# Second half of x turned by transposing transfers instead of TensorE

## The chip, the cores and the metric

The kernel runs on 1 core of one Trainium2 chip. The metric is the time of one execution on the device in microseconds (us). Before the change it is 2121.41 us, the median of 3 runs (2120.31 to 2122.93). Engines: PE is TensorE (matmuls, weight loads apart as PEld), DVE is VectorE, ACT is ScalarE, POOL is GpSimd, SP is SyncE, which here only issues transfers. A "q" behind a name (ACTq) is that engine's issuing of transfers.

## The reference

One layer of an encoder, sequence 1024, width 2048, all in float32:

```
h      = rmsnorm(x, pre_g) * (1 + scale(c)) + shift(c)
proj   = h @ w_in                     # 2048 x 4608: q, k, v, gate_a, u, gate_p
y_a    = windowed_attention(q, k, v) * silu(gate_a)
y_p    = multiscale_pool(u) * silu(gate_p)
g      = sigmoid(h @ w_merge + b_merge)          # 2048 x 4096
merged = g_a * (y_a @ w_branch_attn) + g_p * (y_p @ w_branch_pool)
out    = x + gate(c) * rmsnorm(merged @ w_out, post_g)
```

The change touches how h gets its second half of columns, channels 1024 to 2047: x must be normalised (a factor per row, rstd), turned so that channels lie on partitions, and modulated (a factor and a shift per channel).

## The kernel before

**Products.** Every float32 factor is split into a high part (ACT, L92) and a low part (DVE, L93), and a product is three matmul passes: high x high, high x low, low x high. On top of that the blocks are multiplied by Strassen's scheme (Winograd's form): a pair of 128-column blocks of weights takes seven products, named after the moving operand B11, T3, T2, B21, T4, T1, B22, in the accumulators X, V and Z (L207). Each product is 12 matmuls of 128x512 over four k tiles. A pair of blocks is the unit of the order: `run` goes through its seven pieces and at some of them (`every`) takes one step off a list of side work, `side`.

**Stages.** The input projection with w_in and w_merge goes over 34 pairs, for the first 1024 channels of h first (pass 1), with the partial results in DRAM, and then for the second (pass 2). The first half of x is turned at the start by PE. While pass 1 goes on, its side lists do other work: the modulation vectors, the gate, the bias lines, and sums of w_out's blocks for the last stage (`weight_sums`: four loads, four sums on DVE, four stores to ws_d; `with_sums` puts the loads at one step and the sums three steps on). The last ten pairs of pass 1, from about 535 to 705 us, hold the stage that is changed: x's second half, in 16 tiles of 128 rows x 512 columns, and the weight sums 9 to 15.

**The stage.** In step n tile n is fetched on ACT's queue (L832) and tile n - 5 is turned: ACT scales it by rstd (L837), PE makes four 128x128 transposes into a bank of PSUM (L840), and ACT copies them to H, the stage's buffer of turned x (L841). Then come 16 steps of modulation (L462 on ACT, L464 on DVE), four of preparation (`pre`, L107), and in the last pair the operand fills for pass 2 begin. The weight sums share the ring of eight tiles (`xt2`) with x, and start when its tiles come free.

**Order and queues.** Each engine has one queue and keeps its order. A scheduler orders the instructions by the order of the code. Side steps are put behind the latest matmul and the latest low part by `placed`. Halves of weights (whi, wlo) have four buffers each, so the half for a product is made when the product four earlier lets its buffer go. In a pair ACT also copies X to seed Z (L233) and reads the accumulators (L218, L256, L279). POOL issues the side loads and side stores; SP issues the weights and results of the products.

Of the kernel before, what the change touches and what calls it, by code (L numbers as in the profile page):

```python
# [11 lines left out]

F32 = mybir.dt.float32
F32R = mybir.dt.float32r
AF = mybir.ActivationFunctionType
ALU = mybir.AluOpType
AX = mybir.AxisListType
# [3 lines left out]
P = 128  # L21
# [8 lines left out]
NB = S // P  # L30
# [6 lines left out]
HALF = KT // 2  # L37
# [5 lines left out]
def encoder_layer(ctx: ExitStack, tc: tile.TileContext, x, c, table, w_ada, b_ada, pre_g,  # L43
# [15 lines left out]
    nc = tc.nc  # L59
    x = x[0]  # L60
# [4 lines left out]
    def pool(name, bufs=1, **kw):  # L65
        return tc.tile_pool(name=name, bufs=bufs, reuse_waits="tile", **kw)
# [10 lines left out]
    def uid(s):  # L77
        cnt[0] += 1
        return f"{s}_{cnt[0]}"

    def bank(tag, name="b"):
        return psum.tile([P, 512], F32, tag=tag, name=uid(name), bufs=1 if tag in SEEDED else 2)
# [23 lines left out]
    def sub(o, a, b, eng=None):  # L106
        (eng or nc.vector).tensor_tensor(o, a, b, ALU.subtract)  # L107
# [3 lines left out]
    side_load = side_store = nc.gpsimd.dma_start  # L111

    ident = const.tile([P, P], F32, name="ident")
# [7 lines left out]
    sc = const.tile([P, KT], F32, name="sc")  # L121
# [200 lines left out]
    mid = ExitStack()  # L322
# [8 lines left out]
    for r0, src in ((0, c[0]), (16, b_ada[0, 0:D]), (32, b_ada[0, D:2 * D]),  # L331
                    (48, pre_g[0]), (64, b_merge[0]), (96, pool_scale[0])):
        n = src.shape[0] // P
# [125 lines left out]
    def modulate(eng, t, k):  # L459
        a, b = modc[:, 1, k:k + 1], modc[:, 0, k:k + 1]  # L460
        if eng is nc.scalar:
            eng.activation(t, t, AF.Identity, scale=a, bias=b)  # L462
        else:
            eng.tensor_scalar(t, t, a, b, op0=ALU.mult, op1=ALU.add)  # L464

    op = new_op()
    PAIRS = (NIN + 2 * D) // 256
# [187 lines left out]
    side = deque([lambda: None] * (7 * RAMP))  # L655
# [22 lines left out]
    parts = {}  # L678
# [8 lines left out]
                  if i < RAMP - 1 else None)  # L687
    flush()
    ramp.close()
    xa = mid.enter_context(pool("xa", 5))  # L690
    i = RAMP

    def pass1(n, side, every=(0, 2, 4, 6), then=None):
# [65 lines left out]
    def weight_sums(n, tile_):  # L759

        q, j = n // 4, n % 4
        r0, n0 = (q // 2 * 8 + 2 * j) * P, q % 2 * 512
        t = [[tile_() for _ in range(2)] for _ in range(2)]
        for k in range(2):
            for h_ in range(2):
                side_load(t[k][h_], w_out[r0 + k * P:r0 + (k + 1) * P, h_ * 1024 + n0:h_ * 1024 + n0 + 512])

        def sums():
            (a11, a21), (a12, a22) = t
            sub(a21, a11, a21)  # L770
            sub(a22, a22, a21)
            add(a11, a11, a22)
            sub(a12, a12, a22)
            for n, s_ in enumerate((a11, a21, a12, a22)):
                side_store(ws_d[q][j * P:(j + 1) * P, n * 512:(n + 1) * 512], s_)

        return sums

    def with_sums(steps, first, stride, ns, tile_):

        got = {}

        def begin(f, n):
            got[n] = weight_sums(n, tile_)
            f()

        def end(f, n):
            f()
            got.pop(n)()

        for i_, n in enumerate(ns):
            a, b = first + i_ * stride, first + i_ * stride + 3
            steps[a] = lambda f=steps[a], n=n: begin(f, n)
            steps[b] = lambda f=steps[b], n=n: end(f, n)
        return steps

    steps = [s_ for m in (2, 3) for s_ in modulation_steps(m)]
# [8 lines left out]
    halves = deque()  # L806
    side = deque(with_sums(steps, 14, 6, range(9), in_ring))
# [13 lines left out]
    mid = ExitStack()  # L821
# [1 line left out]
    H = [sp.tile([P, HALF, 512], F32, name=f"H{s}") for s in range(2)]  # L823
    h = {HALF + k: [H[s][:, k] for s in range(2)] for k in range(HALF)}

    def x_tile():
        return sp.tile([P, 512], F32, tag="xt2", name=uid("xt"), bufs=8)

    def fetch_x(si, q):
        xt = x_tile()  # L830
        c0 = 1024 + q * 512
        nc.scalar.dma_start(xt, x[si * P:(si + 1) * P, c0:c0 + 512])  # L832
        return xt

    def turn_x(si, q, xt):
        with tc.issue_after(last_hi[0].ins):
            nc.scalar.activation(xt, xt, AF.Copy, scale=rstd[:, si:si + 1])  # L837
        pt = bank("sc")
        for j in range(4):
            nc.tensor.transpose(pt[:, j * P:(j + 1) * P], xt[:, j * P:(j + 1) * P], ident)  # L840
        nc.scalar.activation(H[si // 4][:, 4 * q:4 * q + 4, (si % 4) * P:(si % 4 + 1) * P],  # L841
                             pt.rearrange("p (k t) -> p k t", k=4), AF.Copy)

    held, AHEAD = {}, 5

    def x_step(n):
        if n < 2 * NB:
            held[n] = fetch_x(n // 2, n % 2)
        if n >= AHEAD:
            turn_x((n - AHEAD) // 2, n % 2 ^ AHEAD % 2, held.pop(n - AHEAD))  # L850

    steps = [lambda n=n: x_step(n) for n in range(2 * NB + AHEAD)]
    steps += [lambda k=k, s=s: modulate((nc.scalar, nc.vector)[s], h[k][s], k) for k in h for s in range(2)]
    h1, h2 = ({j: h[HALF + ktile(kh, j)] for j in range(4)} for kh in range(2))
    t2 = {}

    def pre(j):
        t2[j] = pre_op(j, h1, h2, x_tile)

    steps += [lambda j=j: pre(j) for j in range(4)]  # L860
    every = (0, 1, 3, 4, 6)
    steps += [lambda: None] * (len(every) * (PAIRS - i) - len(steps))
    side = deque(with_sums(steps, 2 * NB + 1, 4, range(9, 16), x_tile))

    def put_all(o, name, h1, h2, t2):
        for j in range(4):
# [21 lines left out]
    side = deque()  # L888
# [730 lines left out]
```

## Time and profile before

| | |
|---|---|
| median of 3 runs | 2121.41 us |
| the profiled execution | 2121.76 us |
| its span, first to last instruction | 2119.6 us |
| PE busy | 2076.9 us, 98% |
| DVE busy | 1502.2 us, 71% |
| ACT busy | 1087.1 us, 51% |
| POOL busy | 195.8 us, 9% |
| mean granted clock of TensorE | 0.998 |

The span is measured inside the execution; 2.2 us lie around it. Durations in the trace are of that one execution. A timeline row merges like instructions: start, length from the first's start to the last's end, and a count; rows of PE overlap, since matmuls are pipelined, so strides between starts say more than lengths.

### The profile page before, as it was taken

Reading aid. Unit: us, or ns where it says so; the run is one execution under the profiler, and the core shown is the slowest. Engines: PE = TensorE matmul, PEld = TensorE weight load, DVE = VectorE, ACT = ScalarE, POOL = GpSimd, SP = SyncE. Lnnn points to the kernel's source line nnn. Section 1 sums busy time; section 2 is a strip of 40 time slices with the busy share of each in tenths; the row PEclk is TensorE's granted clock in tenths of the full one; section 3 lists DMA queues with packets and bytes.
Section 4 is the critical chain, followed back from the end, with each engine's and each line's share of the span. In section 5 each row is a group of like instructions: output and inputs, shape, how many; then the busy total and the mean of one; then the engine's idle time right before and its main releaser. Section 6 shows DMA issues by size and latency. Waiting matters only on the chain.

```text
span 2119.6 us, 28981 instructions
## 1 busy us (share of the span) xinstructions
PE 2076.9 (98%) x9628; PEld 1710.3 (81%) x9628; DVE 1502.2 (71%) x2701; ACT 1087.1 (51%) x2007; POOL 195.8 (9%) x424
## 2 busy tenths in 40 slices
PE   5999999999999999999999999999999999999997
PEld 3688888888888888888888888788888887888886
DVE  6788577775456866777776678757857977556568
ACT  6664444443564636777675333333645645545343
POOL 1402132221022100000000000000000000000012
PEclk9999999999999999999999999999999999999999
DMA  9868688885566565455544676575565646588358
GB/s 343 279 226 311 235 287 293 282 292 172 173 211 230 185 191 185 158 172 186 180 163 147 214 231 209 183 221 177 189 209 184 209 134 203 189 283 288 97 175 306
DMA packets 268390, 455.62 MB, mean 215 GB/s; under 512 B 23594, under 2 KB 119986, under 8 KB 268240
## 3 DMA queue, kind: packets, MB, share of 16 engines
q1 hardware_dynamic: 234016, 345.58, 50.2%
q0 software_dynamic: 30256, 100.85, 14.0%
q10 hardware_dynamic: 3968, 7.34, 1.1%
q8 instruction: 76, 1.25, 0.3%
q14 instruction: 74, 0.61, 0.1%
HBM read 321.53 MB, written 134.24 MB: 215 GB/s over the span
## 4 chain that ended last, share of the span: by engine, by line
PE 92%; DMA 4%; DVE 2%; ACT 1%; issue 1%; DVEq 0%; SPq 0%; ACTq 0%
PE Z L207 31%; PE X L207 21%; PE V L207 21%; PE OUT L1306 13%; DMA ada<-in_w_ada_dram 1%; DMA xt<-in_x_dram 1%; PE PT L987 1%; DVE po L1520 1%; PE SCORE L965 0%; PE SCORE L964 0%; PE SCORE L966 0%; PE PV L999 0%; PE PV L997 0%; PE PV L998 0%; PE GEMV L428 0%
## 5 line engine op out<-in xcount | busy, mean ns | idle before, releaser
L92 ACT ACTIVATE whi<-raw 128x512 fp32r<-128x512 f32 (+1 forms) x537 | 321.0, 601 | 467.8 <-PE Z L207 265.1
L93 DVE TENSOR_TENSOR wlo<-raw,whi 128x512 fp32r<-128x512 f32 (+1 forms) x537 | 348.4, 652 | 139.2 <-PE Z L207 79.4
L93 DVE TENSOR_TENSOR wlo<-wr,whi 128x512 fp32r<-128x512 f32 x112 | 76.5, 689 | 83.7 <-ACT whi L92 83.7
L92 ACT ACTIVATE whi<-wr 128x512 fp32r<-128x512 f32 x112 | 69.9, 628 | 111.2 <-PE OUT L1306 105.4
L104 DVE TENSOR_TENSOR u<-V,u 128x512 f32<-128x512 f32 x90 | 62.1, 690 | 73.6 <-PE V L207 73.2
L92 ACT ACTIVATE whi<-ws 128x512 fp32r<-128x512 f32 (+1 forms) x90 | 54.1, 601 | 106.5 <-PE V L207 104.0
L104 DVE TENSOR_TENSOR raw<-raw,raw 128x512 f32<-128x512 f32 x78 | 53.8, 690 | 70.8 <-DMA raw<-in_w_merge_dram 41.4
L207 PE MATMUL Z<-B22h,whi 128*128 128x512 f32 x334 | 91.3, 392 | 0.7 <-ACT u L256 0.7
L207 PE MATMUL X<-B11h,whi 128*128 128x512 f32 x334 | 91.7, 392 | 0.0
L207 PE MATMUL Z<-T1h,wlo 128*128 128x512 f32 x334 | 90.4, 390 | 1.0 <-DVE wlo L93 1.0
L207 PE MATMUL V<-T4h,whi 128*128 128x512 f32 x334 | 91.3, 392 | 0.0
L207 PE MATMUL V<-T3h,whi 128*128 128x512 f32 x334 | 91.3, 393 | 0.0
L207 PE MATMUL Z<-T1h,whi 128*128 128x512 f32 x334 | 91.3, 391 | 0.0
L207 PE MATMUL V<-T4l,whi 128*128 128x512 f32 x334 | 90.9, 390 | 0.0
L207 PE MATMUL X<-B21h,whi 128*128 128x512 f32 x334 | 90.8, 391 | 0.0
L207 PE MATMUL X<-B11l,whi 128*128 128x512 f32 x334 | 90.8, 390 | 0.0
L207 PE MATMUL Z<-T2h,whi 128*128 128x512 f32 x334 | 90.7, 391 | 0.0
L207 PE MATMUL X<-B11h,wlo 128*128 128x512 f32 x334 | 90.6, 390 | 0.0
L207 PE MATMUL V<-T3h,wlo 128*128 128x512 f32 x334 | 90.6, 390 | 0.0
L207 PE MATMUL Z<-B22l,whi 128*128 128x512 f32 x334 | 90.5, 390 | 0.0
L207 PE MATMUL V<-T3l,whi 128*128 128x512 f32 x334 | 90.5, 390 | 0.0
L207 PE MATMUL X<-B21h,wlo 128*128 128x512 f32 x334 | 90.4, 390 | 0.0
(418 smaller groups left out, 5112.3 us busy)
## 6 DMA issues: line engine op xcount, KB each, us to landing
part<-part_d SPq DMA_DIRECT2D x136, 256.0 KB, 4.1
raw<-in_w_merge_dram SPq DMA_DIRECT2D x64, 512.0 KB, 5.4
raw<-in_w_in_dram SPq DMA_DIRECT2D x60, 512.0 KB, 4.5
ada<-in_w_ada_dram POOLq DMA_DIRECT2D x96, 256.0 KB, 6.2
proj_d<-part SPq DMA_DIRECT2D x68, 256.0 KB, 2.2
gada<-in_w_ada_dram POOLq DMA_DIRECT2D x32, 512.0 KB, 5.8
gt<-proj_d SPq DMA_DIRECT2D x64, 256.0 KB, 3.3
wr<-ws_d SPq DMA_DIRECT2D x32, 512.0 KB, 4.8
```

The source lines that it names most:

```text
L92: last_hi[0] = nc.scalar.activation(hi, src, AF.Copy)
L93: last_split[0] = nc.vector.tensor_tensor(lo, src, f32(hi), ALU.subtract)
L104: (eng or nc.vector).tensor_tensor(o, a, b, ALU.add)
L207: last_mm[0] = nc.tensor.matmul(ps, w_[:, i], op[mov][j][m_], start=fresh and i == 0 and n == 0, stop=i == nj - 1 and n == 2, skip_group_c ...
L987: nc.tensor.transpose(pt[:, i * P:(i + 1) * P], p[:, i * P:(i + 1) * P], ident)
L1306: nc.tensor.matmul(banks[t], m_[:, ts_], w_, start=fresh and j == 0 and n == 0, stop=j == KS - 1 and n == 2, skip_group_check=True)
L1520: last_lo[0] = nc.vector.scalar_tensor_tensor(o_, o_, s_[:, 2:3], rows_x[si][n], op0=ALU.mult, op1=ALU.add)
```

## The change

- A tile of x is now fetched by POOL's queue. ACT scales it as before, then copies it as 16-bit words with the low words of all elements in front of the high ones (a `COPY` of 128 x 2 x 512), and issues a transposing transfer (`DMA_TRANSPOSE`) of those words into a third tile of 128 x 8 x 128 words. DVE joins low and high words back into float32 in H (`join_x`, a copy of 128 x 4 x 128 x 2 words). The transposes on PE and ACT's copy out of PSUM are gone.
- The stage's 50 steps are laid out by a table: tile n is fetched in step 3n/2 (rounded down), turned four steps later, joined two steps after that. Modulation and preparation follow in free steps, the preparation in steps 40 to 43.
- The weight sums 9 to 15 get four tiles of their own (`ws2`), start at step 4 instead of 17 and come every 6 steps instead of 4; the four sums are spread over two steps.
- The ring of side loads in the stage before (`xa`) has seven tiles instead of five, and the DMA scratch of POOL's transfers is 8192 bytes per partition, half of the default.

```diff
-    xa = mid.enter_context(pool("xa", 5))
+    xa = mid.enter_context(pool("xa", 7))
...
-        def sums():
+        def sums(parts=(0, 1)):
             (a11, a21), (a12, a22) = t
-            sub(a21, a11, a21)
-            sub(a22, a22, a21)
+            if 0 in parts:
+                sub(a21, a11, a21)
+                sub(a22, a22, a21)
+            if 1 not in parts:
+                return
             add(a11, a11, a22)
             sub(a12, a12, a22)
...
+    def x_tile(shape=(P, 512), dt=F32):
+        return sp.tile(list(shape), dt, tag="xt2", name=uid("xt"), bufs=8)
...
-    def turn_x(si, q, xt):
+    def fetch_x(n):
+        si, q = n // 8 * 4 + n % 4, n // 4 % 2
+        held[n] = x_tile()
+        side_load(held[n], x[si * P:(si + 1) * P, 1024 + q * 512:1536 + q * 512])
+
+    def turn_x(n):
+
+        si, xt = n // 8 * 4 + n % 4, held.pop(n)
         with tc.issue_after(last_hi[0].ins):
             nc.scalar.activation(xt, xt, AF.Copy, scale=rstd[:, si:si + 1])
-        pt = bank("sc")
-        for j in range(4):
-            nc.tensor.transpose(pt[:, j * P:(j + 1) * P], xt[:, j * P:(j + 1) * P], ident)
-        nc.scalar.activation(H[si // 4][:, 4 * q:4 * q + 4, (si % 4) * P:(si % 4 + 1) * P],
-                             pt.rearrange("p (k t) -> p k t", k=4), AF.Copy)
...
+        words = x_tile((P, 2, 512), U16)
+        nc.scalar.copy(words, xt.bitcast(U16).rearrange("p (n h) -> p h n", h=2))
+        turns[n] = x_tile((P, 8, P), U16)
+        nc.scalar.dma_start(turns[n], words.rearrange("p h n -> p (h n)"), transpose=True)
+
+    def join_x(n):
+        s, q, t0 = n // 8, n // 4 % 2, n % 4 * P
+        nc.vector.tensor_copy(
+            H[s][:, 4 * q:4 * q + 4, t0:t0 + P].bitcast(U16).rearrange("p k (t h) -> p k t h", h=2),
+            turns.pop(n).rearrange("p (h k) t -> p k t h", h=2))
...
+    AHEAD, LAG = 4, 2
+    work = [[] for _ in range(len(every) * (PAIRS - i))]
+    for n in range(16):
+        work[AHEAD + 3 * n // 2 + LAG].append(lambda n=n: join_x(n))
+    for n in range(16):
+        work[AHEAD + 3 * n // 2].append(lambda n=n: turn_x(n))
+    for n in range(16):
+        work[3 * n // 2].append(lambda n=n: fetch_x(n))
...
-    side = deque(with_sums(steps, 2 * NB + 1, 4, range(9, 16), x_tile))
+    side = deque(with_sums(steps, 4, 6, range(9, 16), lambda: sp.tile([P, 512], F32, tag="ws2", name=uid("ws2"), bufs=4), True))
...
-    nc = _bacc.Bacc("TRN2", target_bir_lowering=False, num_devices=1)
+    nc = _bacc.Bacc("TRN2", target_bir_lowering=False, num_devices=1, dynamic_dma_scratch_size=8192)
```

ACT's queue near the first tiles, before: loads of x, scalings, and at the end the first copy out of PSUM (b) to H. Names with "whi" are high halves of weights.

```order
L92 ACTIVATE whi_5301<-raw_4993 128x512
L832 DMA xt_5373<-in_x_dram 128x512
L279 ACTIVATE c_5226<-X_5121 128x512
L92 ACTIVATE whi_5311<-ws_5309 128x512
L837 ACTIVATE xt_5171<-xt_5171,rstd 128x512
L92 ACTIVATE whi_5355<-raw_5147 128x512
L837 ACTIVATE xt_5208<-xt_5208,rstd 128x512
L256 ACTIVATE u_1056_5266<-Z_5122 128x512
L92 ACTIVATE whi_5382<-raw_5148 128x512
L837 ACTIVATE xt_5230<-xt_5230,rstd 128x512
L233 ACTIVATE Z_5273<-X_5272 128x512
L841 ACTIVATE H_5119<-b_5295 128x4x128
```

After: each scaling is followed by the copy of words and the transposing issue.

```order
L852 ACTIVATE xt_5141<-xt_5141,rstd 128x512
L280 ACTIVATE c_5185<-Z_4964 128x512
L854 COPY xt_5277<-xt_5141 128x1024
L856 DMA_TRANSPOSE xt_5279<-xt_5277 128x8x128
L93 ACTIVATE whi_5286<-raw_5147 128x512
L219 ACTIVATE u_1046_5206<-Z_5122 128x512
L852 ACTIVATE xt_5171<-xt_5171,rstd 128x512
L854 COPY xt_5304<-xt_5171 128x1024
L93 ACTIVATE whi_5308<-raw_4993 128x512
L280 ACTIVATE c_5224<-X_5121 128x512
L856 DMA_TRANSPOSE xt_5306<-xt_5304 128x8x128
L93 ACTIVATE whi_5318<-ws_5316 128x512
```

The load and the copy to H are gone from this piece, and each tile has brought a copy of words and an issue behind its scaling, sometimes one right behind the other, sometimes with other instructions between.

DVE's queue at the same place, before: low halves of weights (wlo), combinations of weights (raw, ws), reads of results (u, p).

```order
L93 TENSOR_TENSOR wlo_5302<-raw_4993,whi_5301 128x512
L104 TENSOR_TENSOR u_1046_5206<-V_5123,u_1046_5206 128x512
L93 TENSOR_TENSOR wlo_5312<-ws_5309,whi_5311 128x512
L107 TENSOR_TENSOR ws_5495<-raw_5305 128x512
L104 TENSOR_TENSOR raw_5305<-raw_5305,raw_5306 128x4x128
L93 TENSOR_TENSOR wlo_5356<-raw_5147,whi_5355 128x512
L104 TENSOR_TENSOR p_1041_5169<-p_1041_5169,u_1056_5266 128x512
L93 TENSOR_TENSOR wlo_5383<-raw_5148,whi_5382 128x512
```

After: the first two joins (H<-xt) and the sums of w_out's blocks (ws<-ws) stand between them.

```order
L94 TENSOR_TENSOR wlo_5309<-raw_4993,whi_5308 128x512
L105 TENSOR_TENSOR u_1046_5206<-V_5123,u_1046_5206 128x512
L94 TENSOR_TENSOR wlo_5319<-ws_5316,whi_5318 128x512
L860 COPY H_5119<-xt_5279 128x4x256
L108 TENSOR_TENSOR ws_5500<-raw_5312 128x512
L105 TENSOR_TENSOR raw_5312<-raw_5312,raw_5313 128x4x128
L94 TENSOR_TENSOR wlo_5357<-raw_5147,whi_5356 128x512
L105 TENSOR_TENSOR p_1041_5169<-p_1041_5169,u_1055_5264 128x512
L860 COPY H_5119<-xt_5306 128x4x256
L108 TENSOR_TENSOR ws_1057_5269<-ws_1056_5268,ws_1057_5269 128x512
L108 TENSOR_TENSOR ws_1059_5271<-ws_1059_5271,ws_1057_5269 128x512
L94 TENSOR_TENSOR wlo_5385<-raw_5148,whi_5384 128x512
```

Each join stands ahead of the next pair's weight combinations or low halves, which now come after it.

On PE the sixteen rows of four transposes are gone, and nothing else differs but numbers in names.

## Rows read from the trace of the kernel before

**Rows 1.** The page: engines (busy us, share, instructions); the chain that ended last.

```profile
PE 2076.9 (98%) x9628; PEld 1710.3 (81%) x9628; DVE 1502.2 (71%) x2701; ACT 1087.1 (51%) x2007; POOL 195.8 (9%) x424
...
PE 92%; DMA 4%; DVE 2%; ACT 1%; issue 1%; DVEq 0%; SPq 0%; ACTq 0%
```

**Rows 2.** Table by stage: stretch, length, busy us by engine, clock, DMA share.

```profile
0.00:60.00 60.00, 35.13 (x226) 20.20 (x226) 39.26 (x108) 38.09 (x86) 14.82 (x54) 1.00 1.03 344
535.00:705.00 170.00, 170.00 (x781) 140.67 (x780) 96.91 (x154) 89.98 (x151) 30.36 (x56) 1.00 0.66 211
```

**Rows 3.** Who waited for whom, whole run: us in total, times, longest.

```profile
POOL gada L708 <- DVE gacc L712: 50.8, 14, 5.4
...
PE Z L207 <- DVE wlo L93: 1.0, 1, 1.0
```

**Rows 4.** Timeline of PE: start, us, line, operation, out<-in, shape, count.

```profile
100.82 1.07 PE L428 MATMUL GEMV<-ada,scz 128*32 128x256 f32 x16
...
553.85 0.60 PE L840 MATMUL b<-ident,xt 128*128 128x128 f32 x4
...
557.04 0.60 PE L840 MATMUL b<-ident,xt 128*128 128x128 f32 x4
...
560.25 1.07 PE L207 MATMUL Z<-T2h,whi 128*128 128x512 f32 x4
...
562.97 0.60 PE L840 MATMUL b<-ident,xt 128*128 128x128 f32 x4
...
566.51 1.18 PE L207 MATMUL V<-T4h,whi 128*128 128x512 f32 x4
...
621.37 1.07 PE L207 MATMUL Z<-B22h,whi 128*128 128x512 f32 x4
```

**Rows 5.** The line of the transposes (ns min/median/max, first and last start).

```profile
L840 PE MATMUL b<-ident,xt x64: 270/272/273, 553.9 to 618.5; 128*128 128x128 f32 x64
```

**Rows 6.** ACT's operations, whole run: count, busy us, mean ns; issues: min/median/max.

```profile
L837 ACT ACTIVATE xt<-xt,rstd 128x512 f32<-128x512 f32 x16 | 11.4, 711 | 0.0
...
L841 ACT ACTIVATE H<-b 128x512 f32<-128x512 f32 x16 | 9.4, 588 | 0.0
L92 ACT ACTIVATE phi<-win 128x1024 fp32r<-128x1024 f32 x8 | 8.5, 1061 | 4.7 <-DVE win L1087 4.7
...
L832 ACTq DMA_DIRECT2D xt<-in_x_dram x16: 334/334/444, 535.0 to 585.0; - x16
```

**Rows 7.** Table by stage: the window of the sixteen turns.

```profile
540.00:635.00 95.00, 95.00 (x451) 78.56 (x450) 45.38 (x70) 58.38 (x100) 12.42 (x23) 1.00 0.62 193
```

**Rows 8.** Timeline of ACT in the stage.

```profile
554.34 0.58 ACT L233 ACTIVATE Z<-X 128x512 f32<-128x512 f32 x1
...
556.33 0.63 ACT L92 ACTIVATE whi<-raw 128x512 fp32r<-128x512 f32 x1 [0.89 <-PE V L207]
```

**Rows 9.** Timeline of DVE in the stage.

```profile
557.31 0.69 DVE L93 TENSOR_TENSOR wlo<-raw,whi 128x512 fp32r<-128x512 f32 x1 [1.77 <-PE V L207]
```

**Rows 10.** DVE's operations of 128x1024, whole run: count, busy us, mean ns.

```profile
L455 DVE SCALAR_TENSOR_TENSOR acc<-ada,sc,acc 128x1024 f32<-128x1024 f32 x30 | 38.4, 1280 | 14.7 <-DMA ada<-in_w_ada_dram 14.6
...
L453 DVE TENSOR_SCALAR acc<-ada,sc 128x1024 f32<-128x1024 f32 x2 | 1.5, 748 | 0.0
```

**Rows 11.** Transfers, whole run: issuing queue, count, KB each, median us to landing.

```profile
xt<-in_w_out_dram POOLq DMA_DIRECT2D x28, 256.0 KB, 7.1
...
xt<-in_x_dram ACTq DMA_DIRECT2D x20, 256.0 KB, 3.7
...
bias_d<-line_d ACTq DMA_DIRECT2D x4, 512.0 KB, 8.8
```

**Rows 12.** DMA queues from 535 to 640 us: packets, MB, share of 16 engines.

```profile
q10 hardware_dynamic: 2304, 4.20, 14.0%
```

**Rows 13.** POOL: its first ada loads; its side loads' issues (ns min/median/max).

```profile
52.48 5.93 POOL L412 DMA_DIRECT2D ada<-in_w_ada_dram  x8
...
L766 POOL DMA_DIRECT2D xt<-in_w_out_dram x28: 536/537/653, 588.8 to 696.9; - x28
```

More of the change, by code (lines that the diff above doesn't have):

```diff
@@ L14 @@
 F32R = mybir.dt.float32r
+U16 = mybir.dt.uint16
 AF = mybir.ActivationFunctionType
@@ L777, in weight_sums, with with_sums @@
         return sums
-    def with_sums(steps, first, stride, ns, tile_):
+    def with_sums(steps, first, stride, ns, tile_, halves=False):
         got = {}
@@ L789, in end, with half @@
             got.pop(n)()
+        def half(f, n, part):
+            f()
+            got[n]((part,))
         for i_, n in enumerate(ns):
@@ L793, in with_sums @@
             steps[a] = lambda f=steps[a], n=n: begin(f, n)
-            steps[b] = lambda f=steps[b], n=n: end(f, n)
+            if halves:
+                for k in range(2):
+                    steps[b + k] = lambda f=steps[b + k], n=n, k=k: half(f, n, k)
+            else:
+                steps[b] = lambda f=steps[b], n=n: end(f, n)
         return steps
@@ L824, in encoder_layer @@
     h = {HALF + k: [H[s][:, k] for s in range(2)] for k in range(HALF)}
[L826 to L833, printed above, removed]
-    def turn_x(si, q, xt):
+    def x_tile(shape=(P, 512), dt=F32):
+        return sp.tile(list(shape), dt, tag="xt2", name=uid("xt"), bufs=8)
+    held, turns = {}, {}
+    def fetch_x(n):
[4 more added lines that the diff above has]
+        si, xt = n // 8 * 4 + n % 4, held.pop(n)
         with tc.issue_after(last_hi[0].ins):
             nc.scalar.activation(xt, xt, AF.Copy, scale=rstd[:, si:si + 1])
-        pt = bank("sc")
-        for j in range(4):
-            nc.tensor.transpose(pt[:, j * P:(j + 1) * P], xt[:, j * P:(j + 1) * P], ident)
-        nc.scalar.activation(H[si // 4][:, 4 * q:4 * q + 4, (si % 4) * P:(si % 4 + 1) * P],
-                             pt.rearrange("p (k t) -> p k t", k=4), AF.Copy)
[L844 to L853, printed above, removed]
+        words = x_tile((P, 2, 512), U16)
[7 more added lines that the diff above has]
+            turns.pop(n).rearrange("p (h k) t -> p k t h", h=2))
     h1, h2 = ({j: h[HALF + ktile(kh, j)] for j in range(4)} for kh in range(2))
@@ L858, in pre @@
         t2[j] = pre_op(j, h1, h2, x_tile)
-    steps += [lambda j=j: pre(j) for j in range(4)]
     every = (0, 1, 3, 4, 6)
-    steps += [lambda: None] * (len(every) * (PAIRS - i) - len(steps))
-    side = deque(with_sums(steps, 2 * NB + 1, 4, range(9, 16), x_tile))
+    AHEAD, LAG = 4, 2
[6 more added lines that the diff above has]
+        work[3 * n // 2].append(lambda n=n: fetch_x(n))
+    free = deque([*range(12, 28, 3), *range(29, 39)])
+    for s in range(2):
+        for k in range(HALF):
+            work[free.popleft()].append(lambda k=HALF + k, s=s: modulate((nc.scalar, nc.vector)[s], h[k][s], k))
+    for j in range(4):
+        work[40 + j].append(lambda j=j: pre(j))
+    steps = [lambda fs=fs: [f() for f in fs] for fs in work]
+    side = deque(with_sums(steps, 4, 6, range(9, 16), lambda: sp.tile([P, 512], F32, tag="ws2", name=uid("ws2"), bufs=4), True))
     def put_all(o, name, h1, h2, t2):
```

## The prediction

> **What bounds the kernel now.** I read the engine totals first: TensorE (PE) is busy 98% of the span and the chain that ended last lies on it for 92% [rows 1]. [...] So here PE is the bound. Work taken off PE shortens the run by its full length; work added elsewhere costs nothing until it makes PE wait. Where the waits are added up over the run, the largest of PE at the product line, L207, is a single one of 1.0 us [rows 3].
>
> **What is removed from PE.** Sixteen times four transposes (L840) stand between products. A product without them takes 2.72 us: from 560.25 to 562.97. With them the stride is 3.19 us (553.85 to 557.04) or 3.21 (557.04 to 560.25) [rows 4]. All together: from the first transpose at 553.85 to the end of the product behind the last, 621.37, there are 67.52 us and 22 products, 16 with transposes and 6 without. 22 x 2.72 = 59.84, so the transposes cost 7.68 us, or 0.48 each four. The 64 rows of 0.27 us would sum to 17 us [rows 5]; most of that is overlap in the pipeline, which is why I use the strides. The order of PE differs in nothing else. **Term 1: -7.7 us.**
>
> **What is added to ACT.** Per tile of x (16 in all) ACT loses the copy out of PSUM (0.59 us) and its load's issue (0.33). It keeps the scaling (0.71), and gains a copy that parts the low and high 16-bit words, 1024 elements per partition, and the issue of the transposing transfer [rows 6]. The copy is not in the trace; the ACT rows of 128x1024 take 1.06 us, those of 128x512 about 0.6, and I take 1.06. Between 540 and 635 us, where the sixteen lie, ACT is busy for 58.4 of 95 us [rows 7]. After the change: 58.4 - 16 x 0.59 + 16 x 1.06 = 66.0, in a stretch shorter by 7.7 us, 87.3. That leaves 21.3 us, 1.3 per tile, for the issue and for the wait on ACT's own copy in front of it.
> The issue is not in the trace either. From below: a plain issue on ACT's queue, 0.33 us. From above: one such issue for each of the eight 128x128 blocks of words, 8 x 0.33 = 2.7 us. I take a value near the lower row, under 1.3, since it is one instruction on the same queue. Then ACT keeps up. Should it fall behind for a moment, PE does not see it at once: the copy that seeds Z ends at 554.92 and its product starts at 560.25 [rows 4, 8], 5.3 us, less the two groups of transposes between them, 4.4; the halves of the weights are further ahead (there are four buffers of each, so the half that waited at 556.33 for V<-T3h is for the fourth product on, V<-T4h at 566.51, and DVE's at 557.31 too) [rows 4, 8, 9]. Behind a late transposing issue on ACT stand the next weight half and the next read of PSUM, for which PE waits. **Term 2: 0 us**, hidden behind products.
>
> **What is added to DVE.** Sixteen joins write the words of a tile back into H, 1024 elements each. Their bounds are the 128x1024 rows of DVE, 0.75 us (one input) and 1.28 (two) [rows 10]; I take the upper, since the words are strided. The weight sums of this stage start earlier, so some two more sets of four (0.69 each) fall before 635. DVE: 45.4 + 16 x 1.28 + 8 x 0.69 = 71.4 of 87.3 us [rows 7, 10]. It fits, with 1.0 us per tile to spare.
> A join adds a wait: DVE stands until the transposed tile has landed, and behind it in the queue are low halves of weights. It is queued two steps after its turn. The five steps of a pair lie at pieces 0, 1, 3, 4 and 6 of seven, so two steps are three products, once two: 2.8 on average, 7.6 us. Off that go the scaling, the copy and the issue, 0.71 + 1.06 + 0.33 = 2.1, which leaves 5.5 us for the transfer. The transfer isn't in the trace. From below: the plain loads of x on the same queue land 3.7 us after issue; from above: the slowest of that queue, 8.8 us [rows 11]. I take the lower, a tile of the same 256 KB, with a little on top. Where that meets the short gap of 5.4 - 2.1 = 3.3 us, DVE stands for half a microsecond; its low half is done at 558.00 and its product starts at 566.51, 8.5 us ahead, or 7.5 without the two groups of transposes between [rows 4, 9]. **Term 3: 0 us.**
> [...]
>
> **DMA engines.** The loads of x move from ACT's queue to POOL's at equal bytes. New are 16 transfers of 256 KB. In the window the DMA share is 0.62 [rows 7], so 36 of 95 us are free. ACT's queue moved 4.20 MB in 2304 packets in 14.0% of the 105 us from 535 to 640: 0.92 us for each 256 KB, 6.4 ns a packet [rows 12]. From below, 16 x 0.92 = 15 us, which fits. From above, in pieces of 256 bytes, 1024 packets x 6.4 ns = 6.5 us each, 105 us in all, which doesn't. I take the lower, by bytes. **Term 4: 0 us.**
>
> **The rest.** POOL gets 16 issues at 0.54 us and stands idle for most of the window (12.4 busy of 95) [rows 7, 13]; x is asked for four steps, some 15 us, ahead, against 7.1 us to landing on that queue [rows 11]. Side-load tiles: POOL's waits for their buffers (50.8 us for the gate's alone) shrink, and PE is not behind them [rows 3]; 0 us. [...]
>
> **Sum.** The profiled execution took 2121.76 us (span 2119.6 and 2.2 around it), 0.35 above the median of the timed runs, 2121.41. 2121.76 - 7.68 = 2114.08; by the median 2113.7. I say 2114.0.
>
> **Rivals.**
> *ACT is held by the transposing issue.* One mechanism on ACT's queue: the sequencer stays in the instruction until the words are out, and weight halves and seeds queue up behind it. It decides against the change from (87.3 - 66.0 + 7.7 + 4.4)/16 = 2.1 us per issue. At the upper bound of 2.7: 66.0 + 42.7 = 108.7 us of work in 87.3, 21.4 over, less the 4.4 of lead, 17.0 lost: 2131, slower. For it: the copy just ahead must end first, so nothing of the hold is covered by ACT's own work. Against it: all sixteen x issues on this queue stay at 0.33 to 0.44 us [rows 6].
> *The transposed tiles land late.* With 8.8 us DVE stands 8.8 - 5.5 = 3.3 us per tile, 1.0 of which is spare: 2.3 x 16 = 36.8, less the 7.5 us by which low halves are ahead: 29.3 lost, 2143. It turns the gain around from 5.5 + 1.0 + (7.7 + 7.5)/16 = 7.5 us to landing. For it: DMA engines at 0.62 already, and POOL's transfers need 7.1 [rows 7, 11]. [...]
> *The gain doesn't arrive whole.* ACT and DVE, both fuller, each make PE wait for a part: up to 3.5 us of the 7.7 left or less, 2118 to 2122. For it: DVE goes from 45.4 to 71.4 us in the window, so a late weight load or join has less room to be made good [rows 7]. Against it: leads of 4.4 and 7.5 us, each of which must be used up first.
>
> **How the numbers follow.** Hidden as reckoned: 0.68, with a range of its own of 2112.5 to 2117. Gain in part or none: 0.10. ACT held: 0.11. Late tiles: 0.11. A measurement of this kernel tells 0.2%, 4.2 us, from no change. Faster by more than that (below 2117.2): 0.68 and a little of the third, 0.70. Within it: 0.13, from the third and the mild ends of the two others. Slower: 0.17. The range runs from 2112 to 2121; above it lie most of the two slow cases.
>
> **What would show it.** Right: in the stage every product has a stride of 2.72 us, PE is without idle time, 535 to 705 is shortened by 7.7 us, and no wait of PE for L93's halves or the Z seed has appeared. Term 2 fails if the transposing rows on ACT's queue are longer than 2 us or ACT's busy time meets the stage's length. Term 3 fails if the joins show waits of DVE for the transfers of more than 2 us each. Term 4 fails if the stage's DMA share nears 1 and raw weights come late; the scratch, if POOL's issues after 52 us grow. The forecast as a whole is wrong if PE idles in the stage for more than 3 us.

## The result: 2132.7 us, slower

The changed kernel takes 2132.69 us (median of 6 runs, 2129.76 to 2140.64), the kernel before, run beside it, 2122.41 (6 runs, 2120.31 to 2125.58). The ratio is 1.0057, 95% interval 1.0046 to 1.0067: slower by 10 us at the medians and by 12 by the ratio, where 7.7 us were forecast as a gain. The profiled execution took 2129.97 us, its span is 2127.9, so 8.3 us longer than the span before. It is one of the two quickest of the six: some 3 us of the median's loss are in no trace.

The table by stage of the kernel after answers [rows 2, 7] (stretch, its length, busy us by engine, granted clock, DMA share, GB/s):

```profile
535.00:705.00 170.00, 158.42 (x683) 129.61 (x682) 97.71 (x159) 92.04 (x146) 34.38 (x63) 0.97 0.93 223
540.00:635.00 95.00, 84.56 (x363) 68.53 (x361) 44.65 (x72) 57.66 (x90) 19.02 (x35) 0.97 1.00 213
```

TensorE, busy for the whole of the stage before, now misses 11.6 of 170 us. The DMA share between 540 and 635 has gone from 0.62 to 1.00. VectorE and ScalarE are hardly fuller (97.7 and 92.0 us of the 170, 96.9 and 90.0 before). The waits of TensorE in the stage (total, times, longest) answer [rows 3], where the largest in the product line was 1.0 us:

```profile
PE Z L208 <- DVE wlo L94: 10.9, 2, 6.4
PE V L208 <- ACT whi L93: 0.4, 1, 0.4
PE V L208 <- DVE wlo L94: 0.4, 1, 0.4
```

The two long ones in TensorE's timeline, to be held against [rows 4] (start, length, line, operation, operands, count, idle time before it and its releaser):

```profile
601.72 1.07 PE L208 MATMUL Z<-T2h,whi 128*128 128x512 f32 x4
602.63 1.07 PE L208 MATMUL Z<-T2l,whi 128*128 128x512 f32 x4
608.20 1.88 PE L208 MATMUL Z<-T2h,wlo 128*128 128x512 f32 x4 [4.50 <-DVE wlo L94]
609.88 1.91 PE L208 MATMUL X<-B21h,whi 128*128 128x512 f32 x4
611.58 1.20 PE L208 MATMUL X<-B21l,whi 128*128 128x512 f32 x4
612.62 1.07 PE L208 MATMUL X<-B21h,wlo 128*128 128x512 f32 x4
...
636.14 2.07 PE L208 MATMUL Z<-T2h,wlo 128*128 128x512 f32 x4 [6.36 <-DVE wlo L94]
638.01 1.62 PE L208 MATMUL X<-B21h,whi 128*128 128x512 f32 x4
639.46 1.07 PE L208 MATMUL X<-B21l,whi 128*128 128x512 f32 x4
```

Where nothing waits, groups of four start 0.90 or 0.91 us apart, three to a product: 2.72 us, as Term 1 had it for every product. Behind each long wait the next groups take up to 1.9 and 2.1 us instead of 1.07. The granted clock is 1.00 up to 608 us and 0.50 from 609 to 611, after the engine has stood for 4.5 us; in the second stall, of 6.4 us, it is 0.50 from 633 to 639. From 608.20 to 612.62 there are 4.42 us where three strides are 2.72, so 1.7 lost; from 636.14 to 639.46 another 1.5. Of the 16.0 us lost (7.7 hoped for and 8.3 more), 11.6 are idle time and 3.2 lie in these slow groups, by my reckoning the lower clock. That leaves 1.2, of which each wait explains 0.16 beyond its idle time: a group that flows starts that much before the one ahead of it ends (0.91 apart, 1.07 long).

The whole span hides two more differences, which cancel. Group by group, TensorE is already 3.71 us behind the kernel before at 538 us (538.52 against 534.81 for the same group) and 11.75 at 725 (725.60 against 713.85), so the stage itself is 8.0 us longer; some 3.4 us are won back later. Most of the early loss lies behind 32 matmuls of one column at 510 us, where the clock from 500 to 515 us is 0.93 on average, against 1.00 before. It does not hang on the change: the kernel before with two sums moved (e10 below) has 0.91 there. Single executions differ by such 3 us, which is why the experiments are compared by medians.

What wlo waited for stands in VectorE's timeline:

```profile
606.85 0.69 DVE L105 TENSOR_TENSOR raw<-raw,raw 128x512 f32<-128x512 f32 x1 [8.64 <-DMA raw<-in_w_merge_dram]
607.46 0.68 DVE L94 TENSOR_TENSOR wlo<-raw,whi 128x512 fp32r<-128x512 f32 x1
...
634.79 0.69 DVE L105 TENSOR_TENSOR raw<-raw,raw 128x512 f32<-128x512 f32 x1 [10.30 <-DMA raw<-in_w_merge_dram]
635.40 0.68 DVE L94 TENSOR_TENSOR wlo<-raw,whi 128x512 fp32r<-128x512 f32 x1
```

The sum at L105 belongs to the next pair of weights and needs a raw load. The wlo at 607.46, which TensorE waits for, belongs to the current pair and has its data (TensorE had begun to read its high half at 601.72, and in the second stall at 627.80), but stands behind that sum in VectorE's queue and starts 0.61 us after it. ScalarE is held at a transposing issue in both stalls, so this matters:

```profile
598.54 5.78 ACTq L856 DMA_TRANSPOSE xt<-xt  x1
...
630.67 5.72 ACTq L856 DMA_TRANSPOSE xt<-xt  x1
```

The high halves behind these holds (604.36 and 636.44) are for later products, and TensorE stood before it came to them. When was the raw load issued? SyncE's queue:

```profile
593.99 0.38 SPq L174 DMA_DIRECT2D raw<-in_w_merge_dram  x1
...
621.28 0.38 SPq L174 DMA_DIRECT2D raw<-in_w_merge_dram  x1
```

From issue to the sum there are 12.9 and 13.5 us. Without its wait, TensorE would have begun the product's last third at 602.63 + 0.91 = 603.54, 9.5 us after the issue (8.3 the second time). The kernel before had come close to this once. Its VectorE, SyncE and TensorE:

```profile
621.71 0.69 DVE L104 TENSOR_TENSOR raw<-raw,raw 128x512 f32<-128x512 f32 x1 [7.24 <-DMA raw<-in_w_merge_dram]
622.32 0.69 DVE L93 TENSOR_TENSOR wlo<-raw,whi 128x512 fp32r<-128x512 f32 x1
```

```profile
610.58 0.38 SPq L173 DMA_DIRECT2D raw<-in_w_merge_dram  x1
```

```profile
625.90 1.07 PE L207 MATMUL Z<-T2h,wlo 128*128 128x512 f32 x4
```

There the load took 11.1 us and had 15.3. So two things came together: the load takes some 2 us longer than that slow one, and it is issued 6 to 7 us later against its need. The second comes from the first, in a loop. SyncE issues a raw load when a buffer of raw is free, and that is when VectorE has split it; the waits of SyncE's queue from 535 to 660 us, and VectorE ahead of 593.99:

```profile
SPq L174 <- DVE wlo L94: 35.1, 11, 8.4
```

```profile
580.21 0.69 DVE L105 TENSOR_TENSOR raw<-raw,raw 128x512 f32<-128x512 f32 x1 [6.83 <-DMA raw<-in_w_merge_dram]
...
586.52 0.69 DVE L860 COPY H<-xt 128x1024 uint16<-128x1024 uint16 x1 [3.21 <-DMA xt<-xt]
...
593.28 0.68 DVE L94 TENSOR_TENSOR wlo<-raw,whi 128x512 fp32r<-128x512 f32 x1
```

One pair earlier a raw load came late (6.83 us) and a transposed tile too (3.21); VectorE fell behind, freed the buffer with the wlo at 593.28, and the next load went out at 593.99, too late. The DMA queues from 535 to 660 us (packets, MB, share of 16 engines; issues with KB and median us to landing) answer [rows 11, 12]:

```profile
DMA packets 29305, 27.75 MB, mean 222 GB/s; under 512 B 18168, under 2 KB 23420, under 8 KB 29296
...
q10 hardware_dynamic: 16896, 4.20, 35.5%
q0 software_dynamic: 3679, 12.06, 34.0%
q1 hardware_dynamic: 8721, 11.38, 31.6%
...
raw<-in_w_merge_dram SPq DMA_DIRECT2D x11, 512.0 KB, 6.8
...
xt<-xt ACTq DMA_TRANSPOSE x16, 8.4
```

Queue q10, ScalarE's, moves the same 4.20 MB as before, in 16896 packets instead of 2304: 1056 for each transposing transfer. Its packets take 35.5% of 125 us: 44.4 us, 2.77 per tile, where the plain loads took 0.92 [rows 12]. The three queues sum to 1.01. The first long wait in slices of 2 us shows what that does:

```profile
604.00:606.00 2.00, 0.00 (x0) 0.00 (x0) 0.00 (x0) 1.64 (x3) 0.59 (x2) 1.00 1.30 264
606.00:608.00 2.00, 0.00 (x0) 0.00 (x0) 1.15 (x2) 2.00 (x4) 0.00 (x0) 1.00 1.33 65
608.00:610.00 2.00, 1.80 (x5) 1.41 (x6) 1.35 (x3) 1.72 (x4) 0.00 (x0) 0.61 1.43 59
```

The DMA share is 1.43 here, above one, while 59 GB/s are moved, against 264 at a share of 1.30 four us earlier. So 2.77 us is what a transfer took in this crowd; what it would take alone, no run shows.

The new instructions, as forecast and not: issue of the transposing transfer, ScalarE's copy, VectorE's join.

```profile
L856 ACTq DMA_TRANSPOSE xt<-xt x16: 1247/1347/5778, 545.9 to 648.1; - x16
...
L854 ACT COPY xt<-xt 128x1024 uint16<-128x1024 uint16 x16 | 16.6, 1039 | 1.5 <-DMA xt<-xt 1.3
...
L860 DVE COPY H<-xt 128x1024 uint16<-128x1024 uint16 x16 | 11.1, 692 | 12.8 <-DMA xt<-xt 12.8
```

### The profile page after: what moved, and what is told of

It reads as the page before. It is cut to its first block, busy times and chain, and to the rows that moved or that the text cites. A ratio compares the mean times of both kernels' runs of the same rounds, so it can differ in the third digit from the quotient of the medians.

```text
span 2127.9 us, 28905 instructions
## 1 busy us (share of the span) xinstructions
PE 2075.7 (98%) x9564; PEld 1707.8 (80%) x9564; DVE 1510.6 (71%) x2717; ACT 1093.6 (51%) x2007; POOL 205.2 (10%) x440
## 3 DMA queue, kind: packets, MB, share of 16 engines
q8 instruction: 75, 1.23, 0.2%
## 4 chain that ended last, share of the span: by engine, by line
PE 88%; DMA 7%; DVE 3%; issue 1%; ACT 1%; POOL 0%; DVEq 0%; ACTq 0%; POOLq 0%; SPq 0%
PE Z L208 29%; PE X L208 20%; PE V L208 19%; PE OUT L1329 13%; DMA xt<-in_x_dram 2%; DMA raw<-in_w_merge_dram 1%; PE PT L1010 1%; DMA ada<-in_w_ada_dram 1%; DVE po L1543 1%; DVE wlo L94 1%; PE GEMV L429 1%; DMA xt<-xt 1%; DMA raw<-in_w_in_dram 1%; PE SCORE L987 0%; PE SCORE L988 0%
## 5 line engine op out<-in xcount | busy, mean ns | idle before, releaser
L105 DVE TENSOR_TENSOR raw<-raw,raw 128x512 f32<-128x512 f32 x78 | 53.8, 690 | 95.5 <-DMA raw<-in_w_merge_dram 61.4
L105 DVE TENSOR_TENSOR u<-V,u 128x512 f32<-128x512 f32 x90 | 62.1, 690 | 66.5 <-PE V L208 66.1
L208 PE MATMUL Z<-T2h,wlo 128*128 128x512 f32 x334 | 92.2, 396 | 10.9 <-DVE wlo L94 10.9
L208 PE MATMUL V<-T4h,wlo 128*128 128x512 f32 x334 | 90.3, 390 | 0.4 <-DVE wlo L94 0.4
L208 PE MATMUL X<-B21l,whi 128*128 128x512 f32 x334 | 90.5, 390 | 0.0
L208 PE MATMUL Z<-T1l,whi 128*128 128x512 f32 x334 | 90.5, 389 | 0.0
```

The costliest lines, as they stand in the source:

```text
L105: (eng or nc.vector).tensor_tensor(o, a, b, ALU.add)
L208: last_mm[0] = nc.tensor.matmul(ps, w_[:, i], op[mov][j][m_], start=fresh and i == 0 and n == 0, stop=i == nj - 1 and n == 2, skip_group_c ...
```

## The experiments

The theory from this trace: the transposing transfers crowd the DMA engines, raw loads land late, and TensorE waits through VectorE's queue. Rivals: the weight sums that were brought forward crowd them (S), or ScalarE, held at the issues, is late (H). Times are medians; each ratio is to the kernel before on the same chip (2121.0 to 2121.6).

**1. Same bytes without transposition** (e1).

```diff
-        nc.scalar.dma_start(turns[n], words.rearrange("p h n -> p (h n)"), transpose=True)
+        nc.scalar.dma_start(turns[n].rearrange("p k t -> p (k t)"), words.rearrange("p h n -> p (h n)"))
```

> The changed kernel, with the 16 transposing transfers replaced by plain copies of the same 256 KB from SBUF to SBUF on the same queue (the transposition of the second half of x is left out, so the output is not the reference's); ScalarE's copy, VectorE's join and the order stay. Theory T (the 1056 packets of a transposing transfer, 2.77 us of all 16 DMA engines by the profile, fill the engines, the raw weights land late, and TensorE waits for wlo behind them): the transfers cost about 0.92 us each, the DMA share of 535 to 660 falls below 0.9, the two waits of 4.5 and 6.4 us are gone, and the time is 2114 to 2117. Rival S (the weight sums brought forward fill the engines): little changes, 2127 to 2132.

2112.97 us, ratio 0.9964 (0.9952 to 0.9977). The stage and its queue:

```profile
535.00:705.00 170.00, 170.00 (x751) 140.77 (x751) 108.35 (x175) 100.23 (x157) 35.65 (x64) 1.00 0.73 239
```

```profile
q10 hardware_dynamic: 2304, 4.20, 9.1%
...
raw<-in_w_merge_dram SPq DMA_DIRECT2D x13, 512.0 KB, 5.7
```

TensorE is busy for all 170 us again; a transfer costs 9.1% x 125 / 16 = 0.71 us. Everything else of the change (ScalarE's copy, the joins, early sums, POOL's loads, the scratch) is still there and makes TensorE wait for nothing. S falls as the cause by itself. Between e1 and the changed kernel lie 20 us.

**2. The change without transposing transfers** (e2; the joins go too).

```diff
-        words = x_tile((P, 2, 512), U16)
-        nc.scalar.copy(words, xt.bitcast(U16).rearrange("p (n h) -> p h n", h=2))
-        turns[n] = x_tile((P, 8, P), U16)
-        nc.scalar.dma_start(turns[n], words.rearrange("p h n -> p (h n)"), transpose=True)
+        pt = bank("sc")
+        for j in range(4):
+            nc.tensor.transpose(pt[:, j * P:(j + 1) * P], xt[:, j * P:(j + 1) * P], ident)
+        nc.scalar.activation(H[si // 4][...], pt.rearrange("p (k t) -> p k t", k=4), AF.Copy)
```

> The changed kernel's order, its loads of x on GpSimd's queue, its earlier weight sums and its scratch, but with every tile turned by TensorE and copied by ScalarE as in the kernel before; no transposing transfer. Theory T: the 64 transposes cost TensorE their 7.7 us again and nothing waits, 2121 to 2124. Rival S (the weight sums brought forward alone make the raw weights late): the two waits of TensorE remain beside the transposes, 2128 to 2140.

2121.64 us, ratio 1.0003 (0.9994 to 1.0011), no wait. Against e1 that prices TensorE's transposes: 2121.64 - 2112.97 = 8.7 us, where Term 1 said 7.7.

**3. Weight sums at their old places** (e4).

```diff
-    side = deque(with_sums(steps, 4, 6, range(9, 16), ...
+    side = deque(with_sums(steps, 17, 4, range(9, 16), ...
```

> The changed kernel with the weight sums of the side work begun at step 17 and four steps apart, as in the kernel before, instead of step 4 and six apart. Theory T: the transposing transfers still take 2.77 us each, but the first of them no longer share the engines with the sums' loads and stores; TensorE's waits become smaller and do not all go, 2118 to 2128. Rival S: both waits go, 2112 to 2116.

2133.56 us, ratio 1.0052 (1.0038 to 1.0066). A miss for both: no gain at all. From 535 to 660 us POOL's queue q0 falls to 27.9% and the DMA share to 0.91, yet TensorE waits 9.0 us for wlo at 642. That wlo stands behind a weight sum, whose own load was issued at 628.23 and landed 12.8 us later; a raw load issued at 623.39 took 15.5. The 3.5 us for whi at 709 belong to this edit: the last transposing transfer went out at 636, and VectorE ahead of them waits 5.7 us for a load of the late sums. So this run is no clean test of S, as e1 and e2 are. It shows that a load of w_out can be the late one as well as a raw load, and that a mean share below 1 does not keep TensorE from waiting.

**4. The queue's order** (e5, and e10 as its control in the kernel before).

```diff
-        sub(s3, a11, a21)
+        with tc.issue_after(last_lo[0].ins):
+            sub(s3, a11, a21)
...
-        add(a21, a21, a22)
+        with tc.issue_after(last_lo[0].ins):
+            add(a21, a21, a22)
```

> The changed kernel, with the two weight sums of the next pair that need the raw tiles put behind the current pair's last wlo in VectorE's queue, in every Strassen pair; transfers unchanged. Theory R (the route: wlo of the current pair stands in VectorE's in-order queue behind a sum that waits for a raw load): the waits of 4.5 and 6.4 us go although the DMA engines are as full, 2114 to 2119. Rival B (the engines are simply too full, and whatever comes next waits as long): the waits turn up at the next pair's whi or wlo, 2127 to 2133. Rival W (the order costs the other pairs): VectorE's sums come late in every pair and the time is above 2133.

> The kernel before, with only the two sums of the next pair put behind the current pair's last wlo in VectorE's queue; it is the control for the same edit in the changed kernel, which took 5.8 us from it. If that edit removes a wait that the transposing transfers cause, nothing is won here: 2119 to 2123. If it is a gain of its own: 2113 to 2117.

2126.84 us (1.0030, 1.0019 to 1.0041) with the change, 2122.49 (1.0002, 0.9993 to 1.0010) without. So about 6 of the 20 us hang on that order, and only where the transposing transfers run. What is left waits elsewhere: 3.9 us for a wlo that stands behind a join, which waits 10.26 us for its transposed tile, and 1.9, 1.7 and 0.5 for results of ScalarE. The route matters less than the lateness.

**5. How many packets, or what kind?** (e7, e12).

```diff
-        nc.scalar.dma_start(turns[n], words.rearrange("p h n -> p (h n)"), transpose=True)
+        for b in range(2):
+            nc.scalar.dma_start(turns[n][:, b::2], words.rearrange("p h (k t) -> p (h k) t", t=P)[:, b::2])
```

> The changed kernel, with each transposing transfer replaced by plain copies of the same 256 KB from SBUF to SBUF cut into 1024 pieces of 256 bytes (every second block in each of two transfers; the transposition is left out, so the output is not the reference's). The plain copy in long pieces took all stalls away and ran at 2113.0. Theory N (the number of packets is what costs): about 1024 packets each, 2 us and more of all 16 engines per tile, the raw weights late again, TensorE waits for wlo, 2126 to 2134. Rival X (what costs is the transposition itself, not the size of its pieces): 2112 to 2116, as with long pieces.

> The changed kernel with plain copies in place of the transposing transfers, as in the run with 256-byte pieces, but cut into 2048 pieces of 128 bytes (the transposition is left out, so the output is not the reference's). In 256-byte pieces a tile took 1.17 us of all 16 engines and nothing waited. Theory E (what counts is the engines' time per tile, against the 2.26 us that were free): if 128-byte pieces take 1.2 to 1.7 us per tile, 2113 to 2118; if they take 2.3 us or more, the waits for the raw weights come back and the time is 2122 to 2134. Rival X (a transposing transfer delays others by something else than its engines' time): 2113 to 2118 even at 2.3 us or more.

2115.98 us (0.9975, 0.9965 to 0.9985) in 256-byte pieces and 2116.75 (0.9982, 0.9973 to 0.9990) in 128-byte pieces. The queue rows of e7:

```profile
q10 hardware_dynamic: 16896, 4.20, 15.0%
```

and of e12:

```profile
q10 hardware_dynamic: 33280, 4.20, 22.2%
```

e7 moves exactly the bytes and the packets of the changed kernel, 16896, in 15.0% instead of 35.5%: 1.17 us a tile. Twice the packets take 1.73. So theory N falls: the number of packets explains 0.71 to 1.17, and the step to 2.77 comes from the transposition (and from the crowd that it makes). At 1.73 us a tile the medians show no such loss, so E is not contradicted and not proved either, since 2.3 us was not reached without transposition. e7's trace has no wait of TensorE in the stage; e12's, the slowest of its twelve executions (2122.99 us), has one. The two issues for one tile hold ScalarE for 7.15 us, and TensorE waits for the read of Z that stands behind them:

```profile
595.10 7.15 ACTq L857 DMA_DIRECT2D xt<-xt  x2
```

```profile
602.95 2.08 PE L208 MATMUL Z<-B22h,whi 128*128 128x512 f32 x4 [3.79 <-ACT u L257]
```

So rival H exists, here with plain copies.

**6. Fewer, or further apart** (e3: odd tiles by TensorE as in experiment 2; e8, whose edit stands here in part: two steps apart, fetches, joins and modulation moved to match).

```diff
-        work[AHEAD + 3 * n // 2].append(lambda n=n: turn_x(n))
+        work[AHEAD + 2 * n].append(lambda n=n: turn_x(n))
...
```

> The changed kernel with every second tile turned by TensorE and copied by ScalarE as before, so that 8 transposing transfers remain of 16. Theory T with a threshold (the engines have room for about 2.2 us per tile step and 8 transfers need 1.4): hardly a wait of TensorE, half of the 7.7 us gained, 2117 to 2121. Rival P (the loss is in proportion to the transfers, 11 us for 16): about 2127.

> The changed kernel with its 16 tiles two side steps apart instead of one and a half, so that the same transfers lie over 121 instead of 91 us. Theory T (the engines are overloaded while the tiles come this densely): the DMA share falls below 1, the waits of TensorE shrink, 2116 to 2126. Rival C (each raw load that meets a transposing transfer is late, however far apart these are): the waits are in other places and as long, 2128 to 2135.

e3: 2118.09 us, 0.9984 (0.9975 to 0.9993), one wait of 1.9 us. Eight transfers keep 3.4 of the 8.7 us and TensorE hardly waits, where sixteen lose 20 us against e1: the loss is not in proportion. e8: 2119.63 us, 0.9994 (0.9982 to 1.0006), the longest wait 2.1 us. The queue of e8, with 14 of its tiles in the 125 us:

```profile
q10 hardware_dynamic: 14784, 3.67, 23.2%
```

2.07 us a tile; over all sixteen, from 535 to 720 us, it is 19.2%, 2.22 each. Less dense by a quarter, the same transfers give 13 us back. Room alone does not make a transfer short, though: in e3, where they go out three steps apart instead of one and a half, the eight take 16.2% of the 125 us, 2.5 each. What sets the time of one is open.

**7. ScalarE or the queue?** (e6: issued by SyncE; e13: e1 with ScalarE held longer; e14: e6 with it held longer).

```diff
-        nc.scalar.dma_start(turns[n], words.rearrange("p h n -> p (h n)"), transpose=True)
+        nc.sync.dma_start(turns[n], words.rearrange("p h n -> p (h n)"), transpose=True)
```

```diff
         nc.scalar.copy(words, xt.bitcast(U16).rearrange("p (n h) -> p h n", h=2))
+        nc.scalar.copy(words, xt.bitcast(U16).rearrange("p (n h) -> p h n", h=2))
```

> The changed kernel with the 16 transposing transfers issued from SyncE's queue, where the raw weights and the results are issued, instead of ScalarE's. Rival H (ScalarE, held up to 5.8 us at an issue, makes TensorE wait): the waits go, 2114 to 2119. Theory E (the engines' time): they stay, and the raw loads issue later behind the transposing transfers, 2129 to 2150.

> Plain copies in long pieces in place of the transposing transfers (2113.0 by itself; the transposition is left out, so the output is not the reference's), and ScalarE's copy ahead of each of them done twice, so that ScalarE is held 1.04 us more per tile, 1.5 with the issue, as long as a transposing issue holds it. Rival H (ScalarE's time at the issue is what costs): 2122 to 2132. Theory Q (the transposing packets beside the raw weights on the engines): no more than 2 us, 2112 to 2116.

> The transposing transfers issued from SyncE's queue (2119.6 by itself), and ScalarE's copy ahead of each of them done twice, so that ScalarE loses 1.04 us per tile again, nearly what the issue on its own queue took. Rival H: the waits return, 2127 to 2134. Theory Q: 2118 to 2122, no difference.

e6: 2119.64 us, 0.9989 (0.9980 to 0.9997). This went against theory E's expectation and looked like H. But e13 takes 2114.25 (0.9967, 0.9955 to 0.9979), 1.3 us over e1, and e14 2122.16 (1.0013, 1.0000 to 1.0025), 2.5 over e6. In e14's profiled execution TensorE waits 4.9 and 3.0 us for results of ScalarE, but these stand behind scalings that wait 6.2 and 7.4 us for a tile of x: late loads once more. Both edits add an even 1.04 us per tile, while the sixteen issues of the changed kernel sum to 32.4 us, 2.0 each, with two of over 5.7. The closer control is e12: in its profiled execution 32 issues hold ScalarE for 33.7 us in all, the longest for 5.94, and even that slow execution is 7 us quicker than the changed kernel's; e12's median is 3.8 over e1's. So ScalarE's time costs a few us and not 13, and by elimination the queue is left. That is argued, not shown: e6 also changes when the transfers go out (543.8 to 632.9 us instead of 545.9 to 648.1), and no run holds the two apart. In e6 raw loads and transposing transfers are on SyncE's queue together:

```profile
q1 hardware_dynamic: 26832, 17.04, 58.2%
...
raw<-in_w_merge_dram SPq DMA_DIRECT2D x12, 512.0 KB, 5.6
...
xt<-xt SPq DMA_TRANSPOSE x16, 6.1
```

With some 33% for the raw loads and results, as in the other runs, 25% are left for 16 tiles: 2.0 us each by this estimate, and the raw loads land in 5.6 us at the median instead of 6.8. How an engine shares its time between two queues no row shows; that part is open.

**8. Together** (e9: e3 with experiment 4's order; e11: e8 with it; e15: e8 issued by SyncE).

> Every second tile by a transposing transfer and the others by TensorE (2118.1 by itself), and the two sums of the next pair behind the current pair's last wlo. The first alone left one wait of 1.9 us, for wlo behind a raw load. Theory R (that route is what is left): no wait, 2115 to 2118. Rival (the rest is the clock and the spread of runs): 2118 to 2119, no difference.

> All 16 tiles by transposing transfers, two steps apart (2119.6 by itself), and the two sums of the next pair behind the current pair's last wlo. Theory E with route R: the spread lets the engines keep up and the order takes the remaining wlo wait, 2114 to 2118. Rival: with the engines at a share of 0.93 another load is late in its place, 2119 to 2122.

> The transposing transfers issued from SyncE's queue and two side steps apart instead of one and a half (2119.6 by either edit alone). If both edits take load off the same bursts of the engines, together they leave no wait of over 1 us: 2113 to 2117. If what is left comes from the transposing transfer itself meeting a raw load: 2117 to 2122.

e9 2118.34 us (0.9990, 0.9980 to 0.9999), as e3 alone, though its profiled execution (2116.04) has no wait in the stage. e15 2119.74 (0.9997, 0.9986 to 1.0008), as either edit alone; its one wait over 1 us, 3.5, stands behind a scaling that waits 7.9 us for a tile of x. e11 2126.75 (1.0019, 1.0006 to 1.0033; runs from 2114.8 to 2133.7), a miss: worse than e8. Its one long wait, in VectorE's timeline

```profile
605.78 0.69 DVE L862 COPY H<-xt 128x1024 uint16<-128x1024 uint16 x1 [13.10 <-DMA xt<-xt]
```

and in ScalarE's and TensorE's:

```profile
607.83 1.15 ACT L93 ACTIVATE whi<-raw 128x512 fp32r<-128x512 f32 x2 [11.01 <-DVE raw L108]
...
609.50 0.57 ACT L234 ACTIVATE Z<-X 128x512 f32<-128x512 f32 x1
```

```profile
610.13 2.07 PE L208 MATMUL Z<-T2h,whi 128*128 128x512 f32 x4 [8.60 <-ACT Z L234]
```

goes the other way round: a join waits 13.1 us for a transposed tile, the weight sums stand behind it, the weight half on ScalarE behind those, and the seed of Z behind that. With 16 transposing transfers some load is late in many runs (a transposed tile, raw weights, w_out or x), and the order only chooses who notices. The fastest kernel here that turns all of x is e3, 3.4 us faster than before.

## Why the prediction was wrong

**The step that failed is Term 4.** "I take the lower, by bytes": 0.92 us of all engines per tile, 15 us in all, which fits into 36 free ones. Measured are 2.77 us per tile, 44 in all: nearer the lower bound than the upper (6.5), but over the 36/16 = 2.26 us at which the free time is gone. Nor were 36 us free: the term left out the loads and stores of the weight sums that the change itself brings forward. In e1, where TensorE waits for nothing, the two other queues take from 540 to 635 us

```profile
q1 hardware_dynamic: 8156, 10.48, 36.0%
q0 software_dynamic: 3354, 11.00, 33.5%
```

which leaves 29 us, 1.8 per tile. The bounds held and were far apart; I chose the end at which there was no loss, though an end above 2.26 would have decided, and gave a full DMA no rival of its own. The term's own sign of being wrong came: a share of 1.00 and raw weights late. Small pieces alone would have fitted: at e7's 1.17 us each TensorE waits for nothing in the stage (its median is 3 us over e1's). What the sum lacked is the price of transposing itself, which takes the same packets from 1.17 to 2.77 us in this stage.

In the runs a transposing transfer took 2.77 us of the engines in the changed kernel and 2.22 spread out (e8), against 0.71 for a plain copy of the same bytes in long pieces (e1), 1.17 at 256 bytes (e7) and 1.73 at 128 (e12).

**Term 1 holds**: 7.7 forecast, 8.7 between e2 and e1, and strides of 2.72 us wherever nothing waits.

**Term 2** had the copy right (1.06 against 1.04) and the issue at its limit at the median (1.35 against 1.3) but not on average (2.0, up to 5.78 while the engines are full). Held for as long as that median with plain copies, ScalarE costs 1.3 us (e13), which is within the spread of the runs. The rival of a held ScalarE turned against the change from 2.1 us per issue; it came close to that, but its waits did not come: long holds are seen twice, and both stalls of TensorE end with wlo, behind a raw load. That its 2131 us lie near the measured 2132.7 is chance. That the sequencer stays in the instruction until the words are out, as this rival had it, no row shows: the issues took 1.35 us at the median where the landing took 8.4.

**Term 3** had the joins too dear (1.28 against 0.69) and the landing too quick (3.7 against 8.4 at the median, 18.8 at most). Its rival reckoned 2143 at 8.8 us from waits of the joins, 3.3 us sixteen times; there were 8, 12.8 us in all. VectorE waited longer for raw weights, 8.64 and 10.30 us in the two stalls. I had counted wlo as 7.5 us ahead, from one pair at 557 us; at 622 the lead was already 2.9 (wlo ends at 623.01, its product starts at 625.90), behind a raw load that took 11.1. The prediction has no price for raw loads, only a sign to look for ("raw weights come late"), and not the loop by which one late load delays the issue of the next.

**The rest** is 0 as taken: e2 has POOL's loads, the early sums, seven tiles and half the scratch, and the time of the kernel before. That half the scratch could hold POOL's loads back, no run shows: in the kernel after, with half of it, the 32 loads from 52 us on are issued in 722 ns each at the median, from 52.0 to 79.2 us, and in the kernel before in 722, from 52.5 to 79.5.

**A part of the loss that no case of the prediction had**: TensorE at a granted clock of 0.50 in and after its waits, 3.2 us in the profiled execution.

## What to carry to other kernels

When work is moved to the DMA engines, price it in engine time per transfer, not in bytes (here 0.92 us a tile by bytes and 2.77 measured): take the bound at which the free time is gone, and if the cost may lie on either side of it, that is the forecast's main rival. A mean DMA share near 0.9 does not tell the loss: from 535 to 660 us it is 0.91 in e6, which waits 3.1 us, and in e4, which waits over 10. What told was a late load that work stood behind: 12.9 and 13.5 us from the issue of raw weights to their sum in the two stalls, 12.8 to the landing of w_out in e4. Look for the place where an engine already waits for that load, for what of the current step stands behind it in order, and for whether a late load also delays the issue of the next. Moving half of the transposes won 3.4 us, where moving all of them lost 10.

## What the runs showed of the hardware

- A transposing transfer of 256 KB within SBUF (128 x 1024 words of 16 bits) has 1056 packets and takes 2.0 (e9) to 2.8 us (the changed kernel) of all 16 engines; a plain copy with the same number of packets takes 1.17 (e7).
- Its issue holds the queue for 1.25 us at least (1.23 on SyncE's), and 5.8 in the changed kernel at the most; a plain one in long pieces takes 0.47 (e1). One of 1024 short pieces was held for 5.94 (e12).
- The same transfers on the queue of the loads that they disturb cost 13 us less than on a queue beside it (e6), for a reason that is open.
- VectorE joins 128x1024 words of 16 bits, strided, in 0.69 us; ScalarE parts them in 1.04.
